# Block products of weights that stay in PSUM, sums of weights made by transfers, and six more pairs of products done by blocks

## The chip, the cores and the metric

The kernel runs on one core of one Trainium2 chip. The metric is the device time of one execution in microseconds (us); three executions before the change took 1703.23, 1706.94 and 1707.2 us, a median of 1706.94 us. The engines are TensorE (PE, with its weight loads as PEld), VectorE (DVE), ScalarE (ACT), GpSimd (POOL) and SyncE (SP, which here only issues transfers).

## The reference, cut to what matters

A decoder trunk of two layers runs on 512 prompt tokens and 64 sample tokens (8 sequences of 8), so 576 columns in all, with a model width of 1024 and a branch width of 2048, in float32. Layer 0 is a gated short convolution, layer 1 an mLSTM block. What matters here are the products with weight matrices:

```python
# layer 0
b_gate, c_gate, xa, z = jnp.split(h @ w_in, 4, axis=-1)      # 1024 -> 4 * 2048
u = c_gate * xa
conv, new_buf = causal_dwconv(u, buf, conv_w)
y = b_gate * conv * jax.nn.silu(z)
x = x + y @ w_out                                            # 2048 -> 1024
# layer 1
xm, z = jnp.split(h @ w_in, 2, axis=-1)                      # 1024 -> 2 * 2048
xc = silu(causal_dwconv(xm, ...) + conv_b)
q, k, v = xc @ w_q, xc @ w_k, xm @ w_v                       # 2048 -> 2048 each
...                                                          # gates, chunkwise mLSTM, states
x = x + ((norm(h) * onorm_w + skip * xc) * silu(z)) @ w_out
```

All twelve outputs (both token groups' results, the new convolution states, and the mLSTM's states) are computed by both kernels.

## The kernel before, in words

**Tiles.** Activations lie with the width on the 128 partitions and the 576 tokens along the row. A weight chunk is the weights of 128 output columns for 1024 inputs, 128 x 1024 values (512 KB), loaded as one tile `wr`. Every float32 operand is split in two parts of fewer bits, `hi` (a cast on ACT) and `lo` (the rest, a subtraction on DVE), and a product is three matmuls: hi by hi, hi by lo, lo by hi. `split_weights` (lines 208 and 209) and `parts_of` (lines 256 and 257) do this for weights, half a chunk (128 x 512) at a time, into rings of four `wh` and four `wl` tiles.

**Plain products.** `products` (matmuls on line 228) multiplies one chunk with 8 input tiles: 8 x 3 x 2 = 48 matmuls, since the 576 tokens are done as 256 and 320 columns.

**Block products.** `block_pair` (matmuls on line 310) does two chunks at once by Winograd's form of Strassen's method. The two chunks by the two halves of the input tiles are four weight blocks a11, a12, a21, a22; the inputs are cut the same way, by halves of the tiles and of the tokens (288 each), and their sums t1 to t4 are made once (`mixed`). Seven products of 12 matmuls with 288 columns, 84 in all, take the place of the 96 of two plain products. The sums of weights are made on DVE: s1 = a21 + a22 and s2 = s1 + a11 (lines 292 and 293), a21 + a11 (line 326) and s2 + a12 (line 331). Four PSUM banks of the tag `blk` hold the products; between them, results go to SBUF and are combined there by additions on DVE (lines 322 to 359).

**Layer 0.** A loop runs over 16 width tiles f. In each, the gate and input chunks of the next tile (4f+4 and 4f+5) are done by `block_pair`; then the last two chunks of this tile, 4f+2 for z and 4f+3 for the output gate, by two plain products (`product(2)` and `product(3)`). The convolution's steps of the tile stand in a list `work` and are let in between the blocks. In layer 0, tiles of the tag `X` (7 buffers) hold the sums and intermediate results; the loads have 4 `wr` buffers.

**Layer 1.** After the projection, `gemm_pair` computes v (8 pairs) and then k and q (16 pairs): for each pair a block product of 84 matmuls for the lower 1024 inputs, and two calls of `plain` (line 369), 48 matmuls each, which add the upper 1024 inputs in the same PSUM banks. `then` names the next pair, whose weights are loaded and summed from within this one. Behind these come the mLSTM's chunks, the z products and the output product; `block_pair` has no part in them.

**What sets the order.** The program is written in one order, and a scheduler that models the time of each instruction puts each engine's queue in order when the kernel is built. Each queue is then worked through in order, with semaphore waits. SP's queue issues the loads of the weights, in order too: a load that waits for its buffer holds up the ones behind it.

Of the kernel before, what the change touches and what calls it, by code (L numbers as in the profile page):

```python
# [57 lines left out]
AHEAD = 2  # L58
FH = 2
FI = 1  # L60
EARLY = 3.45
# [6 lines left out]
def trunk(tc, io):  # L68
    nc = tc.nc
    ctx = ExitStack()  # L70
    with ctx:
# [150 lines left out]
        def step(acc, w, xs, k, first, last, parts=HALVES):  # L222
# [3 lines left out]
            for p, (a, x) in enumerate(((hi, xh), (hi, xl), (lo, xh))):  # L226
                for i, j, o in parts:
                    nc.tensor.matmul(acc[:, o:o + j - i], a[:, k % 4, :], x[:, i:j], start=(first and k == 0 and p == 0),  # L228
                                     stop=(last and k == 7 and p == 2))

        def products(acc, w, xs, first, last, pops=(), parts=HALVES, hook=None):


            fence = nullcontext
            for k in range(8):
                if hook and hook[0] == k:
                    ins = hook[1]()
                    fence = lambda: tc.issue_after(ins)
                with fence():
                    step(acc, w, xs, k, first, last, parts)  # L240
                if k in pops:
                    run()
                tick(0.735 if len(parts) == 2 else 0.36)

# [37 lines left out]

        ahead_of = {}

        def block_weights(c1, c2):

            r1, r2 = weight_tile(), weight_tile()
            for r, c_ in ((r1, c1), (r2, c2)):
                latest[0] = load(out=r, in_=io["wts"][c_]).ins
            a11, a12, a21, a22 = [r[:, i:8:2, :] for r in (r1, r2) for i in range(2)]  # L290
            s1, s2 = [X(512, name="ws").rearrange("p (k x) -> p k x", x=P) for _ in range(2)]
            nc.vector.tensor_tensor(s1, a21, a22, ALU.add)
            nc.vector.tensor_tensor(s2, s1, a11, ALU.add)
            ahead_of[c1, c2] = a11, a12, a21, a22, s1, s2

        def block_pair(c1, c2, fs, xs, out1, out2, add, mid=None, then=None, pops=0):

            a11, a12, a21, a22, s1, s2 = ahead_of.pop((c1, c2))  # L300
            o11, o12, o21, o22 = out1[:, 0:HT], out1[:, HT:NT], out2[:, 0:HT], out2[:, HT:NT]
# [15 lines left out]
            nc.scalar.copy(p, b0)  # L317
            run(pops)
            b2 = block("p5")
            product(b2, parts_of(s1), "t1", True)  # L320
            if add:
                tt(o12, o12, b1, ALU.subtract)
                tt(o12, o12, p, ALU.add)
            else:
                tt(o12, p, b1, ALU.subtract)
            tt(a21, a21, a11, ALU.add)
            product(b1, parts_of(a21), "t3", False)
            run(pops)
            tt(u, b1, p, ALU.subtract)
            product(b0, parts_of(a12), "b21", False)  # L330
            tt(s2, s2, a12, ALU.add)
            if add:
                tt(o22, o22, b2, ALU.subtract)
                tt(o22, o22, u, ALU.add)
            else:
                tt(o22, u, b2, ALU.subtract)
            run(pops)
            b3 = block("p4")
            product(b3, parts_of(a22), "t4", True)
            run(pops)  # L340
            product(b2, parts_of(s2), "b22", False)
            if mid:
                mid()
            if then:
                block_weights(*then)
            if add:
                tt(o11, o11, b0, ALU.add)
                tt(o21, o21, b3, ALU.add)
                tt(o21, o21, u, ALU.add)
            elif xs is None:  # L350
                nc.scalar.copy(o11, b0)
                tt(o21, b3, u, ALU.add)
            else:
                plain(b3, b1, c2 + 1, xs, False)
                tt(o21, b3, u, ALU.add)
                tt(o22, b1, o22, ALU.add)
                plain(b0, b2, c1 + 1, xs, None)
                nc.scalar.copy(o11, b0)
            tt(o12, o12, b2, ALU.add)

        def plain(ba, bb, chunk, xs, start):

            w = weights(chunk)
            for k in range(8):
# [6 lines left out]
                if k % 2:  # L371
                    run()
                    drip()

        def gemm_pair(c1, c2, fs, xs, out1, out2, plain_first=False, mid=None, then=None):
# [159 lines left out]
        for f in range(NW):  # L535
# [17 lines left out]

            zb = [raw_weights(4 * f + i) for i in (2, 3)] if f else None
            if f + 1 < NW:
                cx = [X(name="cx") for _ in range(2)]
            if f == 0:
                for i in range(2):
                    acc = mm("acc")
                    products(acc, weights(4 + i), h1, True, True)  # L560
                    nc.scalar.copy(cx[i], flat(acc))
                    if i:
                        block_weights(8, 9)
                    first_blocks(2 + i)
                accumulators("acc0a", bufs=2)
            elif f + 1 < NW:
                block_pair(4 * f + 4, 4 * f + 5, fs, None, *cx, False, pops=1)
# [15 lines left out]
            nc.vector.tensor_tensor(cv, product(3), cv, ALU.mult)  # L583
            nc.vector.tensor_tensor(cv, cv, z, ALU.mult)
# [34 lines left out]
        for f in range(NW):  # L619
# [4 lines left out]
            if f < 2:  # L624
                u = raws[f]
                nc.vector.tensor_tensor(u, u, rb, ALU.mult)
            else:
                acc = gemm(80 + f, 1, h2)
                u = T(name="xm")
                nc.vector.tensor_tensor(u, flat(acc), rb, ALU.mult)  # L630
            us.append(u)
# [70 lines left out]
        xc, fc = [], []  # L702
        accumulators("acc1", bufs=4)

        def later_tile(f):
# [3 lines left out]

        def mixed_blocks():  # L710
            for j in range(4):
                fc.append(forms(later_tile(2 * j), later_tile(2 * j + 1)))

        for h in range(NH):
            vt = []
            for dt in (0, 2):
                f = 4 * h + dt
                pair = [T(name="v") for _ in range(2)]
                gemm_pair(96 + 2 * f, 98 + 2 * f, fm, xm, *pair, mid=mixed_blocks if f == NW - 2 else None,
                          then=(100 + 2 * f, 102 + 2 * f) if f < NW - 2 else (176, 178))  # L720
# [98 lines left out]
        for h in (3, 0, 1, 2):  # L819
            st = heads[h]  # L820
            for dt in range(4):
# [11 lines left out]
                if (h, dt) == (2, 3):  # L833
                    xs = []
                gemm_pair(128 + 4 * f, 130 + 4 * f, fc, xc, k, q, plain_first=(h, dt) == (3, 0),
                          mid=next_stage if (h, dt) == (2, 3) else None,
                          then=next(((128 + 4 * g, 130 + 4 * g) for i, g in enumerate(order) if i and order[i - 1] == f), None))
# [676 lines left out]
def _arrays(a):  # L1514
# [91 lines left out]
```

## Time and profile before

| | us |
|---|---|
| median of three executions | 1706.94 |
| the profiled execution's own time | 1710.66 |
| its span, from the first to the last instruction | 1708.8 |
| PE busy | 1670.7 (98% of the span) |
| DVE busy | 1094.3 (64%) |
| ACT busy | 682.3 (40%) |
| POOL busy | 102.3 (6%) |

A busy PE says little on how well it is used, since the matmuls overlap; the time from one matmul's start to the next's says more. The profile's chain of waits follows the work back from the end of the kernel, so a stage in which it names PE alone is one in which nothing but the number of matmuls and their rate sets the time. Line numbers (L310) are those of the kernel before; the same matmuls stand on L332 in the changed one, `parts_of` on L268 and L269 and `plain` on L407.

### The profile page before, as it was taken

What the parts mean: (1) busy time and instruction counts of PE and PEld (TensorE: products, weight loads), DVE (VectorE), ACT (ScalarE), POOL (GpSimd) and SP (SyncE); (2) the same over time, 40 slices, a digit from 0 to 9 for tenths busy, and PEclk for the clock granted to TensorE, in tenths of its full rate; (3) what the DMA queues carried; (4) which work ended last, traced back from release to release, by engine and by line L of the source; (5) the groups of instructions that cost most, each with busy time, mean ns of one, the idle gap of its engine ahead of it and who ended that gap; (6) DMA issues with size and microseconds to landing.
All of it is one profiled execution on the core that took longest, in us unless ns stands there. A gap on an engine that the chain in (4) does not pass through costs nothing.

```text
span 1708.8 us, 30842 instructions
## 1 busy us (share of the span) xinstructions
PE 1670.7 (98%) x12315; PEld 1592.4 (93%) x12315; DVE 1094.3 (64%) x2040; ACT 682.3 (40%) x1252; POOL 102.3 (6%) x241
## 2 busy tenths in 40 slices
PE   9999999999999999999999999999999998997998
PEld 9999999999999999999999989899898787997998
DVE  6977777774436986556856346345368567776775
ACT  5433343342323553433534223233245455554431
POOL 0000000000001000000110110000012000000000
PEclk9999999999999999999999999999999899998999
DMA  5223322224432434445433453542746587897993
GB/s 194 74 80 103 101 89 81 94 74 137 131 121 87 145 111 150 130 133 163 139 93 121 178 181 96 201 160 75 248 153 200 183 284 272 300 341 259 325 332 105
DMA packets 107487, 275.23 MB, mean 161 GB/s; under 512 B 11056, under 2 KB 33456, under 8 KB 107344
## 3 DMA queue, kind: packets, MB, share of 16 engines
q1 hardware_dynamic: 91984, 255.95, 45.4%
q10 hardware_dynamic: 15360, 17.32, 3.0%
q8 instruction: 97, 1.59, 0.4%
q14 instruction: 46, 0.38, 0.1%
HBM read 211.13 MB, written 62.09 MB: 160 GB/s over the span
## 4 chain that ended last, share of the span: by engine, by line
PE 89%; DMA 5%; DVE 3%; ACT 1%; issue 1%; POOL 1%; SPq 0%; DVEq 0%; ACTq 0%
PE acc L228 35%; PE p L310 24%; PE p L369 16%; DMA c<-cs 2%; PE qa L768 2%; DMA cs_out<-c 2%; PE cp L1183 1%; PE r L1129 1%; PE cp L1184 1%; PE g L669 1%; PE ta L688 1%; PE blk L369 1%; PE s L787 1%; DMA wr<-wts 1%; PE s L788 0%
## 5 line engine op out<-in xcount | busy, mean ns | idle before, releaser
L228 PE MATMUL acc<-hi,wh 128*128 128x256 f32 (+1 forms) x1520 | 331.5, 298 | 6.6 <-ACT num L1196 3.6
L208 ACT CAST wh<-wr 128x512 fp32r<-128x512 f32 x286 | 175.9, 620 | 390.9 <-PE acc L228 193.8
L228 PE MATMUL acc<-lo,wh 128*128 128x256 f32 (+1 forms) x1520 | 328.6, 297 | 0.0
L228 PE MATMUL acc<-hi,wl 128*128 128x256 f32 (+1 forms) x1520 | 328.5, 297 | 0.0
L310 PE MATMUL p<-hi,wh 128*128 128x288 f32 x968 | 286.1, 298 | 4.3 <-ACT wh L256 2.1
L310 PE MATMUL p<-lo,wh 128*128 128x288 f32 x968 | 284.4, 295 | 0.0
L209 DVE TENSOR_TENSOR wl<-wr,wh 128x512 fp32r<-128x512 f32 x286 | 194.1, 687 | 137.8 <-ACT wh L208 131.0
L310 PE MATMUL p<-hi,wl 128*128 128x288 f32 x968 | 277.9, 296 | 0.0
L228 PEld LDWEIGHTS acc<-hi,wh 128*128 128x128 f32 x1520 | 256.9, 190 | 12.5 <-ACT num L1196 3.8
L228 PEld LDWEIGHTS acc<-lo,wh 128*128 128x128 f32 x1520 | 255.9, 190 | 1.9 <-issue 1.7
L228 PEld LDWEIGHTS acc<-hi,wl 128*128 128x128 f32 x1520 | 255.9, 190 | 0.4
L310 PEld LDWEIGHTS p<-hi,wh 128*128 128x128 f32 x968 | 181.9, 188 | 7.4 <-ACT wh L256 3.9
L310 PEld LDWEIGHTS p<-lo,wh 128*128 128x128 f32 x968 | 182.4, 188 | 0.0
L310 PEld LDWEIGHTS p<-hi,wl 128*128 128x128 f32 x968 | 179.7, 189 | 1.9 <-issue 1.7
L256 ACT CAST wh<-wr 128x512 fp32r<-128x512 f32 x152 | 94.3, 621 | 217.7 <-PE p L369 97.9
L369 PE MATMUL p<-hi,wh 128*128 128x288 f32 x736 | 168.5, 299 | 0.0
L369 PE MATMUL p<-hi,wl 128*128 128x288 f32 x736 | 167.2, 297 | 0.0
L369 PE MATMUL p<-lo,wh 128*128 128x288 f32 x736 | 165.4, 295 | 0.0
L257 DVE TENSOR_TENSOR wl<-wr,wh 128x512 fp32r<-128x512 f32 x152 | 104.6, 688 | 53.1 <-ACT wh L256 52.1
L257 DVE TENSOR_TENSOR wl<-ws,wh 128x512 fp32r<-128x512 f32 x114 | 78.6, 689 | 89.3 <-ACT wh L256 82.1
L256 ACT CAST wh<-ws 128x512 fp32r<-128x512 f32 x114 | 70.7, 620 | 154.5 <-PE p L369 69.4
L369 PEld LDWEIGHTS p<-hi,wh 128*128 128x128 f32 x736 | 120.4, 188 | 12.6 <-issue 9.4
(367 smaller groups left out, 2542.4 us busy)
## 6 DMA issues: line engine op xcount, KB each, us to landing
wr<-wts SPq DMA_DIRECT2D x222, 512.0 KB, 3.9
c<-cs SPq DMA_DIRECT2D x112, 512.0 KB, 6.1
cs_out<-c SPq DMA_DIRECT2D x64, 512.0 KB, 6.9
x<-xT SPq DMA_DIRECT2D x16, 288.0 KB, 4.2
xcs<-xc ACTq DMA_DIRECT2D x16, 288.0 KB, 2.1
x<-xcs SPq DMA_DIRECT2D x16, 288.0 KB, 4.7
ld<-xcs SPq DMA_DIRECT2D x16, 288.0 KB, 7.2
cp_out<-cp ACTq DMA_DIRECT2D x16, 257.0 KB, 7.2
```

The source lines that it names most:

```text
L208: last_act[0] = nc.scalar.copy(hi, raw[:, 4 * i:4 * i + 4, :]).ins
L209: nc.vector.tensor_tensor(lo, raw[:, 4 * i:4 * i + 4, :], hi.bitcast(F32), ALU.subtract)
L228: nc.tensor.matmul(acc[:, o:o + j - i], a[:, k % 4, :], x[:, i:j], start=(first and k == 0 and p == 0), stop=(last and k == 7 and p == 2))
L256: last_act[0] = nc.scalar.copy(hi, src).ins
L257: nc.vector.tensor_tensor(lo, src, hi.bitcast(F32), ALU.subtract)
L310: nc.tensor.matmul(bank_, a[:, j, :], x, start=(start and j == 0 and i == 0), stop=(j == 3 and i == 2), skip_group_check=True)
L369: nc.tensor.matmul(b, a[:, k % 4, :], x[:, t:t + HT], start=bool(new) and k == 0 and i == 0, stop=(k == 7 and i == 2), skip_group_check=True)
L669: nc.tensor.matmul(g[32 * j:32 * j + 32, 0:b - a], w[:, 32 * j:32 * j + 32], tiles[j][:, a:b], start=True, stop=True)
L688: nc.tensor.transpose(pa[:, 128 * it:128 * it + 128], t[:, 128 * it:128 * it + 128], ident)
L768: nc.tensor.matmul(st["q"][32 * g:32 * g + 32, :], st["qp"][dt // 2][:, dt % 2, 128 * u + 32 * g:128 * u + 32 * g + 32], ct[g // 2][:, g % ...
L787: nc.tensor.matmul(sb[0], a[:, 0:128], b[:, 0:512], **ends)
L1129: nc.tensor.matmul(r, kst[2 * i + j][:, 128 * dt:128 * dt + 128], vst[:, 0:512], start=True, stop=True)
```

## The change

Four things are changed.

1. **Chained products.** The products of a pair are put in another order, and the partial sums stay in PSUM. ACT writes the negative of the first product (a11 by b11) into a second bank, and three further products accumulate there one after another; ACT copies the partial sums out in between (`u`, then `p`, or the fourth bank `bv` where plain products follow). DVE makes two subtractions with results in place of five operations. Since a matmul that is to add onto what ACT wrote needs the bank to have been written by a matmul before, `mark` writes all four banks once by four matmuls of 288 columns where a new set of banks is opened: in layer 0 and ahead of layer 1's v.
2. **Sums by transfers.** For all pairs but the first of layer 0 and the first of layer 1 (`FIRST`), s1 is made by a load of a21 (SP) and an accumulating transfer of a22 onto it (POOL's queue), and a21 + a11 by an accumulating transfer of a11 onto a21. DVE still makes s2 = s1 + a11 and s2 + a12. The accumulating transfers are issued later than the loads (`settle`). The chunks of block products are stored in another order in HBM, so that a block is one piece.
3. **Six tiles' last two products by blocks.** In the width tiles 3, 5, 7, 9, 11 and 13 of layer 0 (`SECOND`), the chunks 4f+2 and 4f+3 are done by a second `block_pair` and no longer by two plain products.
4. **Small things.** The result tiles `cx` come from the large pool for f under 11; the last two projection tiles of layer 1 leave PSUM by an ACT copy; a job between two pairs (`mixed_blocks`) is let in in four pieces.

```diff
+FIRST = (8, 96)
+SECOND = tuple(range(3, 14, 2))
...
+        add_load = nc.gpsimd.dma_start
...
+        def settle():
+            while unsettled:
+                unsettled.pop(0)()
...
         def block_weights(c1, c2):
             r1, r2 = weight_tile(), weight_tile()
             for r, c_ in ((r1, c1), (r2, c2)):
                 latest[0] = load(out=r, in_=io["wts"][c_]).ins
-            a11, a12, a21, a22 = [r[:, i:8:2, :] for r in (r1, r2) for i in range(2)]
+            a11, a12, a21, a22 = [r[:, i:i + 4, :] for r in (r1, r2) for i in (0, 4)]
             s1, s2 = [X(512, name="ws").rearrange("p (k x) -> p k x", x=P) for _ in range(2)]
-            nc.vector.tensor_tensor(s1, a21, a22, ALU.add)
-            nc.vector.tensor_tensor(s2, s1, a11, ALU.add)
+            if c1 in FIRST:
+                nc.vector.tensor_tensor(s1, a21, a22, ALU.add)
+                nc.vector.tensor_tensor(s2, s1, a11, ALU.add)
+                nc.vector.tensor_tensor(a21, a21, a11, ALU.add)
+            else:
+                load(out=s1, in_=io["wts"][c2][:, 0:4, :])
+                def sums():
+                    add_load(out=s1, in_=io["wts"][c2][:, 4:8, :], accum_op=ALU.add)
+                    add_load(out=a21, in_=io["wts"][c1][:, 0:4, :], accum_op=ALU.add)
+                    nc.vector.tensor_tensor(s2, s1, a11, ALU.add)
+                unsettled.append(sums)
...
-            b1 = block("p6")
-            product(b1, parts_of(s2), "t2", True)
-            b0 = block("p1")
-            product(b0, parts_of(a11), "b11", True)
-            nc.scalar.copy(p, b0)
...
+            bx = block("p1")
+            product(bx, parts_of(a11), "b11", True)
+            by = block("p6")
+            nc.scalar.activation(by, bx, AF.Copy, scale=-1.0)
+            bw = block("p5")
+            product(bw, parts_of(s1), "t1", True)
+            m5 = X(HT, name="m5")
+            nc.scalar.copy(m5, bw)
+            product(by, parts_of(s2), "t2", False)
+            nc.scalar.copy(u, by)
+            tt(s2, s2, a12, ALU.add)
+            product(bx, parts_of(a12), "b21", False)
+            product(by, parts_of(a21), "t3", False)
+            if xs is None or add:
+                nc.scalar.copy(p, by)
+            else:
+                bv = block("p7")
+                nc.scalar.copy(bv, by)
+            product(bw, parts_of(s2), "b22", False)
+            product(by, parts_of(a22), "t4", False)
...
+            if xs is None:
+                tt(o22, p, m5, ALU.subtract)
+                nc.scalar.copy(o11, bx)
+                tt(o12, bw, u, ALU.subtract)
+                nc.scalar.copy(o21, by)
+                return
+            plain(bx, bw, c1 + 1, xs, None)
...
+        def mark(w, x):
+            for b in [block("mark") for _ in range(4)]:
+                nc.tensor.matmul(b, w, x, start=True, stop=True)
...
+            second = f in SECOND
+            if second:
+                block_weights(4 * f + 2, 4 * f + 3)
...
-            za = product(2)
             z = T(name="z")
+            if second:
+                b_ = T(name="b")
+                block_pair(4 * f + 2, 4 * f + 3, fs, None, z, b_, False)
+                za = z
+            else:
+                za = product(2)
             nc.vector.tensor_tensor(z, za, rb, ALU.mult)
...
+    blk = [c for c in range(64) if (c // 4 in SECOND if c % 4 > 1 else c >= 8)] + list(range(96, 192, 2))
+    wts[blk] = wts[blk][:, :, [0, 2, 4, 6, 1, 3, 5, 7]]
```

How the queues' order moves is shown at three places. The first is PE's queue in layer 0, in width tile f = 3, where the pair of the next tile ends and the work on z and the output gate begins. Before (`p6183` is a bank of the pair, `acc198` the accumulator of z):

```order
L310 MATMUL p6183_1250<-hi109_664,wh189_1306 128x288
L310 MATMUL p6183_1250<-lo110_665,wh189_1306 128x288
L310 MATMUL p6183_1250<-hi109_664,wl189_1307 128x288
L228 MATMUL acc198_1393<-hi14_137,wh199_1394 128x256
L228 MATMUL acc198_1393<-hi14_137,wh199_1394 128x320
L228 MATMUL acc198_1393<-lo15_138,wh199_1394 128x256
```

and now (`p6191` belongs to the pair of the next tile, `p1207` is the first bank of the new second pair):

```order
L332 MATMUL p6191_1286<-hi109_665,wh197_1347 128x288
L332 MATMUL p6191_1286<-lo110_666,wh197_1347 128x288
L332 MATMUL p6191_1286<-hi109_665,wl197_1348 128x288
L332 MATMUL p1207_1417<-hi14_137,wh208_1418 128x288
L332 MATMUL p1207_1417<-lo15_138,wh208_1418 128x288
L332 MATMUL p1207_1417<-hi14_137,wl208_1419 128x288
```

Where 96 matmuls of line 228 stood, 84 of 288 columns stand. The second place is POOL's queue in layer 0, in which before nothing stood but one small copy for each width tile (`cpa`):

```order
L547 COPY cpa_501<-u83_504 128x2
L547 COPY cpa_501<-u114_691 128x2
L547 COPY cpa_501<-u145_966 128x2
L547 COPY cpa_501<-u176_1241 128x2
L547 COPY cpa_501<-u208_1519 128x2
```

and in which now the accumulating transfers stand between them (L310 and L311 are lines of the changed kernel; `ws` is s1, `wr` the chunk that holds a21):

```order
L587 COPY cpa_501<-u149_977 128x2
L310 DMA ws169_1125<-wts 128x512
L311 DMA wr168_1122<-wts 128x512
L310 DMA ws184_1260<-wts 128x512
L311 DMA wr183_1257<-wts 128x512
L587 COPY cpa_501<-u180_1254 128x2
L310 DMA ws202_1408<-wts 128x512
L311 DMA wr201_1405<-wts 128x512
```

Each of these waits on POOL for the loads of the tiles onto which it adds. The third place is ACT's queue at the new second pair of f = 3, as it is now (`wh` are casts of weights, `p6209` is the bank that is chained, `pu206` and `m5212` take its partial sums and the fifth product's, and `cx187`, a result of the pair before, its last):

```order
L268 CAST wh214_1473<-wr182_1256 128x512
L338 ACTIVATE p6209_1434<-p1207_1417 128x288
L268 CAST wh215_1489<-wr183_1257 128x512
L377 COPY cx187_1264<-p6191_1286 128x288
L268 CAST wh216_1506<-ws185_1261 128x512
L343 COPY m5212_1453<-p5210_1436 128x288
L268 CAST wh217_1522<-wr183_1257 128x512
L346 COPY pu206_1416<-p6209_1434 128x288
L268 CAST wh229_1563<-wr200_1404 128x512
```

Between two copies out of, or into, a bank stands one cast of a later product's weights in most places; before, a pair had two such copies on ACT in all, and now it has six.

More of the change, by code (lines that the diff above doesn't have):

```diff
@@ L242, in products @@
                     run()
+                if k == 5 and unsettled:
+                    settle()
                 tick(0.735 if len(parts) == 2 else 0.36)
@@ L346, in block_pair @@
             if add:
[L347 to L359, printed above, removed]
+                tt(p, p, m5, ALU.subtract)
+                tt(o22, o22, p, ALU.add)
+                tt(o12, o12, u, ALU.subtract)
+                tt(o12, o12, bw, ALU.add)
+                tt(o11, o11, bx, ALU.add)
+                tt(o21, o21, by, ALU.add)
+                return
[4 more added lines that the diff above has]
+                nc.scalar.copy(o21, by)
+                return
+            plain(bx, bw, c1 + 1, xs, None)
+            nc.scalar.copy(o11, bx)
+            if mid:
+                nc.scalar.copy(o12, bw)
+            tt(o12, o12 if mid else bw, u, ALU.subtract)
+            for go in mid[2:3]:
+                go()
+            plain(by, bv, c2 + 1, xs, None)
+            nc.scalar.copy(o21, by)
+            if mid:
+                nc.scalar.copy(o22, bv)
+            tt(o22, o22 if mid else bv, m5, ALU.subtract)
+            for go in mid[3:]:
+                go()
+        def mark(w, x):
+            for b in [block("mark") for _ in range(4)]:
+                nc.tensor.matmul(b, w, x, start=True, stop=True)
         def plain(ba, bb, chunk, xs, start):
@@ L552, in trunk @@
             work.append(saved)
-            zb = [raw_weights(4 * f + i) for i in (2, 3)] if f else None
+            second = f in SECOND
+            if second:
+                block_weights(4 * f + 2, 4 * f + 3)
+            zb = [raw_weights(4 * f + i) for i in (2, 3)] if f and not second else None
             if f + 1 < NW:
-                cx = [X(name="cx") for _ in range(2)]
+                cx = [T(name="cx") if f < 11 else X(name="cx") for _ in range(2)]
             if f == 0:
@@ L577, in product @@
                 return flat(acc)
-            za = product(2)
             z = T(name="z")
+            if second:
[4 more added lines that the diff above has]
+                za = product(2)
             nc.vector.tensor_tensor(z, za, rb, ALU.mult)
             nc.scalar.activation(z, z, AF.Silu)
-            nc.vector.tensor_tensor(cv, product(3), cv, ALU.mult)
+            nc.vector.tensor_tensor(cv, b_ if second else product(3), cv, ALU.mult)
             nc.vector.tensor_tensor(cv, cv, z, ALU.mult)
@@ L629, in trunk @@
                 u = T(name="xm")
-                nc.vector.tensor_tensor(u, flat(acc), rb, ALU.mult)
+                if f < NW - 2:
+                    nc.vector.tensor_tensor(u, flat(acc), rb, ALU.mult)
+                else:
+                    nc.scalar.copy(u, flat(acc))
+                    nc.vector.tensor_tensor(u, u, rb, ALU.mult)
             us.append(u)
@@ L708, in later_tile, with mixed_blocks @@
             return x
-        def mixed_blocks():
-            for j in range(4):
-                fc.append(forms(later_tile(2 * j), later_tile(2 * j + 1)))
+        def mixed_blocks(j):
+            fc.append(forms(later_tile(2 * j), later_tile(2 * j + 1)))
         for h in range(NH):
@@ L718, in trunk @@
                 pair = [T(name="v") for _ in range(2)]
-                gemm_pair(96 + 2 * f, 98 + 2 * f, fm, xm, *pair, mid=mixed_blocks if f == NW - 2 else None,
+                gemm_pair(96 + 2 * f, 98 + 2 * f, fm, xm, *pair, mid=[lambda j=j: mixed_blocks(j) for j in range(4)] if f == NW - 2 else None,
                           then=(100 + 2 * f, 102 + 2 * f) if f < NW - 2 else (176, 178))
```

36 lines of the change are left out of this document (12 added, 24 removed).

## Prediction

> **What bounds the kernel now.** I read the head of the page first, with the shares of the chain of waits by engine.
>
> ```profile
> span 1708.8 us, 30842 instructions
> PE 1670.7 (98%) x12315; PEld 1592.4 (93%) x12315; DVE 1094.3 (64%) x2040; ACT 682.3 (40%) x1252; POOL 102.3 (6%) x241
> PE 89%; DMA 5%; DVE 3%; ACT 1%; issue 1%; POOL 1%; SPq 0%; DVEq 0%; ACTq 0%
> ```
>
> PE carries 89% of the chain. Next come four stretches in the view of windows: twelve width tiles of layer 0, layer 1's v pairs, its k and q pairs, and the rest.
>
> ```profile
> core 0: us, PE busy (x) PEld busy (x) DVE busy (x) ACT busy (x) POOL busy (x), PEclk, DMA share, GB/s
> 101.25:387.16 285.91, 285.91 (x2154) 285.91 (x2154) 215.69 (x380) 112.63 (x192) 7.00 (x12) 1.00 0.29 89
> 612.00:833.40 221.40, 219.70 (x1697) 216.15 (x1697) 146.86 (x281) 93.41 (x166) 11.69 (x33) 1.00 0.45 143
> 833.40:1290.00 456.60, 453.08 (x3394) 417.64 (x3398) 231.69 (x409) 150.76 (x272) 52.37 (x129) 1.00 0.46 150
> 1290.00:1708.80 418.80, 393.37 (x2713) 357.62 (x2707) 289.10 (x584) 193.70 (x409) 16.28 (x36) 0.96 0.76 261
> ```
>
> In layer 0 PE is busy for all of 285.91 us at full clock: only fewer or shorter matmuls help there. The 677 us of v, k and q hold 5.2 us in which PE is free. Last, the chain in one width tile of layer 0, where the pieces are start, length, line and count:
>
> ```profile
> 101.25 9.52 PE p L310 x72
> 110.77 4.92 PE acc L228 x37
> 115.69 1.59 PE p L310 x12
> 117.28 7.88 PE acc L228 x59
> ```
>
> A pair by blocks is 9.52 + 1.59 = 11.11 us for 84 matmuls (0.132 us each), the two plain products are 4.92 + 7.88 = 12.80 us for 96. Together they are the tile's 23.91 us.
>
> **Second pairs.** Six tiles lose 96 matmuls each and gain 84: 12.80 - 11.11 = 1.69 us, times 6 is **-10.14 us**, if the second pair runs as close as the first. Lower bound of the gain 0 (the pair waits for its weights as long as it saves), upper bound the sum itself.
>
> **Opening of the first pair.** This is the one place ahead of layer 0's loop where PE stands still. The timeline on PE and ACT, and three windows behind it:
>
> ```profile
> 48.41 0.42 PE L228 MATMUL acc<-hi,wl 128*128 128x256 f32 x2
> 50.91 0.40 PE L310 MATMUL p<-hi,wh 128*128 128x288 f32 x1 [2.08 <-ACT wh L256]
> 48.87 0.64 ACT L561 COPY cx<-acc 128x576 f32<-128x576 f32 x1 [1.92 <-PE acc L228]
> 50.90:52.80 1.90, 1.89 (x8) 1.25 (x9) 1.90 (x4) 1.90 (x4) 0.00 (x0) 1.00 0.03 9
> 52.80:56.30 3.50, 3.50 (x17) 3.50 (x16) 3.50 (x7) 0.81 (x2) 0.10 (x1) 0.51 0.01 2
> 56.30:57.00 0.70, 0.70 (x8) 0.70 (x7) 0.43 (x1) 0.21 (x1) 0.48 (x1) 1.00 0.00 0
> ```
>
> Before, the pair opens with the sum s2, behind two additions and a cast. Now it opens with a11 and b11, which need no sum; only the four marks wait for the copy `cx`, which ends at 49.51. Four marks are 4 x 0.132 = 0.53 us, so the first product starts near 50.1 in place of 50.91: **-0.8 us**. After the stall the clock is granted at 0.51 for 3.5 us, 3.5 x 0.49 = 1.7 us lost. Whether a shorter stall spares it no row shows: between 0 and -1.7 I take half, **-0.85**.
>
> The Trainium skill (TensorE: Matmul & The Clock Gate, Part 1) has the clock fall only after a whole idle window of about 3.4 us. This trace disagrees, since it fell after 2.08 us. By the page the new, shorter stall could cost nothing, and the sum would be 0.85 us lower.
>
> **Marks ahead of v.** Here PE waits for the last projection tile:
>
> ```profile
> 611.25 0.77 DVE xm L630
> 612.16 9.76 PE p L310 x72
> ```
>
> The new ACT copy (0.64 us by `cx` above) stands ahead of that multiplication, but the marks need only the first tile and may fill the wait. Between 0 and +0.53 I take **+0.53**. The banks are then in use; later pairs have no marks.
>
> **Sums by transfers.** 42 pairs get a third load on SP and two transfers on POOL in place of two additions on DVE. No transfer that adds stands in the trace; the nearest rows are loads in layer 0 (first) and transfers of 256 KB among layer 1's k and q, median us to landing last; and POOL's small operations:
>
> ```profile
> wr<-wts SPq DMA_DIRECT2D x51, 512.0 KB, 3.6
> kps<-ta ACTq DMA_DIRECT2D x15, 256.0 KB, 3.2
> far<-S SPq DMA_DIRECT2D x3, 256.0 KB, 6.5
> ld<-vps SPq DMA_DIRECT2D x1, 256.0 KB, 10.1
> L547 POOL COPY cpa<-u 128x2 f32<-128x2 f32 x12 | 7.0, 584 | 276.6 <-DVE u L544 276.6
> L744 POOL TENSOR_TENSOR qm<-q,nst 128x64 f32<-128x64 f32 x16 | 13.8, 860 | 307.1 <-DVE q L356 284.1 <-DVE q L334 23.0
> L293 DVE TENSOR_TENSOR ws<-ws,wr 128x512 f32<-128x512 f32 x11 | 7.6, 692 | 0.4
> L256 ACT CAST wh<-wr 128x512 fp32r<-128x512 f32 x47 | 29.2, 622 | 57.0 <-PE acc L228 39.3 <-PE p L310 17.7
> ```
>
> The new chain is: chunk load 3.6, load of s1 behind it at most 3.6, POOL's issue 0.58 to 0.86, the transfer A, DVE's s2 0.69, ACT's cast 0.62: 9.4 us + A by the longer values. By the queues' order there lie, in some 18 pairs of layer 0, at least 123 matmuls between the last one that the load waits for and the first that needs what stands behind the sum: 123 x 0.132 = 16.3 us. So A may take 6.9 us before PE waits. Bounds for A are 3.2 and 10.1; layer 0's DMA share is 0.29 against 0.46 where the long ones are, so I take the 3.6 of its own loads: **0**, hidden behind the preceding pair's matmuls. At 10.1 it would be 18 x 3.2 = 57 us. In layer 1 the distances are longer, but for one (105 matmuls, 13.9 us, at the first k and q pair); the third load stands there on SP ahead of the `c` loads, for which PE waits 2.5 us now:
>
> ```profile
> PE qa L768 <- DMA c<-cs: 2.5, 3, 1.4
> ```
>
> Doubled that is +2.5; fewer DVE operations could give back at most the 5.2 us; between these I take 0.
>
> **Chained products.** DVE loses work, ACT gains four operations in a pair. Rows of layer 0:
>
> ```profile
> L317 ACT COPY pu<-p 128x288 f32<-128x288 f32 x12 | 4.7, 393 | 0.0
> L438 ACT ACTIVATE cv<-u,cols 128x576 f32<-128x576 f32 x12 | 9.3, 774 | 0.0
> L352 DVE TENSOR_TENSOR cx<-p,pu 128x288 f32<-128x288 f32 x12 | 5.4, 450 | 0.0
> L257 DVE TENSOR_TENSOR wl<-wr,wh 128x512 fp32r<-128x512 f32 x47 | 32.2, 685 | 1.8 <-ACT wh L256 0.8
> ```
>
> Each of these copies has one whole product, 12 matmuls or 1.59 us, between its bank's last matmul and the next one that adds there. A copy with one operation ahead of it on ACT is at most 0.77 + 0.39 = 1.17 us, which is covered; with two, 0.77 + 0.62 + 0.39 = 1.79 us, it is 0.2 us late, and behind the waiting matmul stand all others. ACT is busy 112.63 of 285.91 us, 39%, so I take **0**; three late copies in each of 44 pairs would be 3 x 44 x 0.2 = 26 us.
>
> **DVE where it is densest.** A second tile has 22.22 us (two pairs) in place of 23.91. DVE's 215.69 us over 285.91 are 18.04 in a tile. Four subtractions for plain weights go (-2.74), seven for blocks come (+4.80), the first pair loses two sums (-1.37) and three of five 288-wide operations (-1.35), the second brings two sums (+1.37) and two subtractions (+0.90): 19.65 of 22.22 us, 88%. It fits, with little room.
>
> **The last stage** (1290 on) has none of these products. Only its order on the queues moves a little; I take 0, with 2 us either way.
>
> **Sum.** -10.14 - 0.8 - 0.85 + 0.53 = **-11.26 us**. The profiled execution took 1710.66 us, 1.86 over its span, and stands 3.72 above the median; so 1699.40 for it, and **1695.7** for the median.
>
> **Rivals.**
>
> *R1, the sums come late (slower).* Layer 0, some 18 pairs: it decides from A = 6.9 us on. For it speak the rows of 6.5 and 10.1 us at the same size; against it the light DMA there and the 3.2. At 10.1 us: 1695.7 + 57 = 1753; at 7.5 it would still be 1706.5.
>
> *R1b, POOL's issue is held up by DVE.* If POOL could prepare a transfer only while DVE is free, 12% of a second tile, its 0.86 us would become 0.86 / 0.12 = 7.2, the chain 15.7 us + A, and with A = 3.6 PE would wait 3.0 us: x 18 = 54, some 1750. Against it: the small POOL copy takes 584 ns beside a DVE that is busy 75%. The Trainium skill (SBUF — State Buffer, The "DVE blocks DMA" trap) states such a lock, for DVE's two-port modes; no run here shows it yet.
>
> *R2, copies late on the chained bank (slower).* Price above: 1695.7 + 26 = 1722. For it: more ACT operations in the same bank's path; against it: ACT's 39%.
>
> *R3, the second pairs give nothing.* With DVE at 88%, the `lo` parts come when the matmuls want them, and the tile keeps its 23.91 us: 1695.7 + 10.14 = 1705.8. For it: the density; against it: DVE's idle time in layer 0 waits for ACT and PE, not the reverse.
>
> *R4, more gain.* The whole clock loss (-0.85) and most of the 5.2 us of PE's free time in v, k and q: some 1690.
>
> **How the numbers follow.** A measurement tells 0.3% from no change, so faster is under 1701.8 and slower over 1712.1. Forecast 0.64 (1691 to 1701.8), R4 0.06: faster 0.70. R3 0.13, all of it within: same 0.13. R1 0.09, R1b 0.03, R2 0.05: slower 0.17. The range is 1689 to 1709: it holds the forecast, R3 and most of R4, and leaves out the slower cases, 0.17, as its remainder. Their prices begin near nothing, so some of them would fall inside as well.
>
> **What would show it.** In the changed profile: two pairs of 84 in width tiles 3, 5, ... 13 with PE unbroken, such a tile 22.2 us long where a plain one stays at 23.9; PE's groups fewer by 64 matmuls; the first pair's stall under 1.3 us and the window behind it at a clock over 0.51; the transfers `ws<-wts` on POOL's queue landing under 6.9 us; no wait of PE on ACT for the chained bank over 0.2 us. I am wrong if layer 0's twelve tiles show PE idle by more than 2 us for `ws`, for the bank's copy or for `wl`; the releaser named there tells R1, R2 and R3 apart.

## The result and the profile after

The changed kernel is slower by 0.4%: a median of 1713.4 us against 1706.68 (15 executions each), a ratio of 1.0037 with a 95% interval of 1.0027 to 1.0047. Forecast were 1695.7 us, in a range of 1689 to 1709. In a second series, on chip 11, the ratio came to 1.0030 (1.0016 to 1.0045).

The head of the profile after (1711.83 us, 1.6 under its median, where before's 1710.66 stood 4.0 over its own) still shows PE as the chain, with the share of transfers up from 5% to 8%:

```profile
span 1710.1 us, 31151 instructions
PE 1673.2 (98%) x12251; PEld 1583.8 (93%) x12251; DVE 1026.3 (60%) x1873; ACT 749.8 (44%) x1463; POOL 168.6 (10%) x325
PE 86%; DMA 8%; DVE 3%; ACT 2%; issue 1%; SPq 1%; POOL 0%; DVEq 0%; ACTq 0%
```

Layer 0 did what was forecast. In the chain of the changed kernel's first dense tiles, 240 block matmuls follow one another without a gap (a pair, the second pair, and six of the seven products of the next tile's pair), and two width tiles take 144.97 - 98.82 = 46.15 us where two took 47.82 before:

```profile
98.82 31.76 PE p L332 x240
130.58 3.59 PE acc L231 x27
134.16 1.59 PE p L332 x12
135.76 9.21 PE acc L231 x69
144.97 31.76 PE p L332 x240
```

Layer 1's first block product comes at 602.05 us (before: 612.16). The 10.1 us are gone again when v, k and q are done. Here is that stage, from the first block product to the last gate product, as the view of windows has it, before and then after:

```profile
612.16:1294.30 682.14, 677.08 (x5132) 636.85 (x5132) 380.44 (x692) 244.73 (x438) 63.97 (x162) 1.00 0.46 149
```

```profile
602.05:1296.21 694.16, 688.63 (x5120) 637.21 (x5119) 320.69 (x550) 274.61 (x539) 94.99 (x207) 1.00 0.58 171
```

It is 12.0 us longer with 12 matmuls fewer, at full clock, and PE is busy for 11.6 us more of it. So it isn't idle time, which goes from 5.1 to 5.5 us: the same instructions take longer. The groups by line tell which; first before, then after (busy us, mean ns, waits):

```profile
L768 PE MATMUL qa<-c,qp 128*32 128x512 f32 x192 | 25.6, 604 | 2.5 <-DMA c<-cs 2.5
L669 PE MATMUL g<-k,wif 128*32 128x256 f32 (+1 forms) x64 | 8.1, 417 | 0.0
L669 PE MATMUL g<-v,wif 128*32 128x256 f32 (+1 forms) x64 | 4.7, 412 | 0.3 <-DVE tb L693 0.3
L669 PE MATMUL g<-q,wif 128*32 128x256 f32 (+1 forms) x64 | 4.7, 412 | 0.0
```

```profile
L821 PE MATMUL qa<-c,qp 128*32 128x512 f32 x192 | 30.8, 605 | 2.2 <-DMA c<-cs 2.1
L722 PE MATMUL g<-k,wif 128*32 128x256 f32 (+1 forms) x64 | 11.5, 416 | 0.0
L722 PE MATMUL g<-v,wif 128*32 128x256 f32 (+1 forms) x64 | 6.4, 415 | 0.0
L722 PE MATMUL g<-q,wif 128*32 128x256 f32 (+1 forms) x63 | 4.9, 413 | 0.0
```

Neither line was edited. `qa` is the query's product with the states, `g` the gates' product; both use 32 of the array's columns (128*32), four of them side by side. They grew by 5.2 and 5.3 us, 10.5 of the 12.0. The timeline shows why (a *run* of small matmuls is here a row of them on PE with no other matmul between). Before, eight `qa` in a row take 1.06 us and sixteen `g` 1.18:

```profile
965.92 1.06 PE L768 MATMUL qa<-c,qp 128*32 128x512 f32 x8
678.51 1.18 PE L669 MATMUL g<-v,wif 128*32 128x256 f32 x16
```

In the changed kernel large matmuls stand between them, and a run of two costs what a run of eight did:

```profile
959.97 1.06 PE L821 MATMUL qa<-c,qp 128*32 128x512 f32 x6
963.26 1.04 PE L821 MATMUL qa<-c,qp 128*32 128x512 f32 x2
660.56 0.63 PE L722 MATMUL g<-v,wif 128*32 128x256 f32 x4
662.89 0.63 PE L722 MATMUL g<-v,wif 128*32 128x256 f32 x4
664.17 0.73 PE L722 MATMUL g<-v,wif 128*32 128x320 f32 x2
670.86 0.74 PE L722 MATMUL g<-v,wif 128*32 128x320 f32 x6
```

In PE's order there are 38 runs of `qa` for 33 in the whole kernel and 28 of `g` for 19. In v, k, q alone `qa` has 29 runs for 24, and the number of runs accounts for its whole growth: 24 runs of 1.06 to 1.07 us are the 25.6 us of before, 29 are the 30.8 of now. The scheduler lets a small product in where its inputs are ready by its model, and the changed pair has its results ready at other times; which part of the change broke the runs is tested below, while the model's own times are not on record.

### The profile page after: what moved, and what is told of

It is laid out like the page before. It is cut to its first block, busy times and chain, and to the rows that moved or that the text cites. A ratio compares the mean times of both kernels' runs of the same rounds, so it can differ in the third digit from the quotient of the medians.

```text
span 1710.1 us, 31151 instructions
## 1 busy us (share of the span) xinstructions
PE 1673.2 (98%) x12251; PEld 1583.8 (93%) x12251; DVE 1026.3 (60%) x1873; ACT 749.8 (44%) x1463; POOL 168.6 (10%) x325
## 4 chain that ended last, share of the span: by engine, by line
PE 86%; DMA 8%; DVE 3%; ACT 2%; issue 1%; SPq 1%; POOL 0%; DVEq 0%; ACTq 0%
PE acc L231 29%; PE p L332 28%; PE p L407 16%; DMA cs_out<-c 2%; PE qa L821 2%; DMA wr<-wts 2%; DMA c<-cs 2%; PE r L1182 1%; PE g L722 1%; PE cp L1236 1%; PE cp L1237 1%; PE ta L741 1%; PE s L840 1%; DMA ws<-wts 1%; PE s L841 0%
## 5 line engine op out<-in xcount | busy, mean ns | idle before, releaser
L332 PE MATMUL p<-hi,wh 128*128 128x288 f32 x1136 | 337.0, 297 | 0.8 <-ACT p L355 0.4
L332 PE MATMUL p<-hi,wl 128*128 128x288 f32 x1136 | 334.7, 295 | 0.7 <-DVE wl L269 0.7
L332 PE MATMUL p<-lo,wh 128*128 128x288 f32 x1136 | 334.4, 295 | 0.0
L231 PE MATMUL acc<-hi,wh 128*128 128x256 f32 (+1 forms) x1328 | 290.0, 299 | 5.7 <-ACT num L1249 2.4
L231 PE MATMUL acc<-lo,wh 128*128 128x256 f32 (+1 forms) x1328 | 288.8, 298 | 0.0
L231 PE MATMUL acc<-hi,wl 128*128 128x256 f32 (+1 forms) x1328 | 288.2, 298 | 0.0
L231 PEld LDWEIGHTS acc<-hi,wh 128*128 128x128 f32 x1328 | 224.7, 191 | 11.5 <-issue 2.6
L231 PEld LDWEIGHTS acc<-hi,wl 128*128 128x128 f32 x1328 | 224.2, 191 | 2.1 <-issue 1.7
L231 PEld LDWEIGHTS acc<-lo,wh 128*128 128x128 f32 x1328 | 224.5, 191 | 0.8 <-issue 0.6
L332 PEld LDWEIGHTS p<-hi,wl 128*128 128x128 f32 x1136 | 212.9, 188 | 3.2 <-issue 2.1
L407 PE MATMUL p<-hi,wh 128*128 128x288 f32 x736 | 161.4, 300 | 0.0
L407 PE MATMUL p<-hi,wl 128*128 128x288 f32 x736 | 160.3, 297 | 0.0
L407 PE MATMUL p<-lo,wh 128*128 128x288 f32 x736 | 159.2, 295 | 0.0
```

What stands on the lines that cost most here:

```text
L332: nc.tensor.matmul(bank_, a[:, j, :], x, start=(start and j == 0 and i == 0), stop=(j == 3 and i == 2), skip_group_check=True)
L407: nc.tensor.matmul(b, a[:, k % 4, :], x[:, t:t + HT], start=bool(new) and k == 0 and i == 0, stop=(k == 7 and i == 2), skip_group_check=True)
```

## The experiments

Two theories stand against each other at first: O, that the order of the small products in layer 1 took the gain; and S, that the sums by transfers come late and hold PE up. Every kernel's stages are read from its trace: "start" to layer 1's first block product, "v, k, q" to the last gate product, "last" to the end of the span. The ratio is to the kernel before on the same chip.

| kernel | ratio (95%) | start | v, k, q | last |
|---|---|---|---|---|
| before | 1 | 612.2 | 682.1 | 414.5 |
| changed | 1.0037 (1.0027 to 1.0047) | 602.0 | 694.2 | 413.8 |
| changed, again | 1.0030 (1.0016 to 1.0045) | 601.8 | 692.5 | 411.3 |
| no second pairs | 1.0106 (1.0080 to 1.0132) | 611.4 | 693.9 | 416.1 |
| before with second pairs | 0.9987 (0.9972 to 1.0003) | 614.0 | 680.3 | 410.9 |
| layer 0 only | 0.9932 (0.9911 to 0.9952) | 603.3 | 680.3 | 406.6 |
| glued | 0.9978 (0.9962 to 0.9993) | 605.2 | 681.6 | 415.4 |
| glued, fourth head as it was | 0.9962 (0.9947 to 0.9977) | 603.5 | 682.3 | 409.0 |
| old form with transfers in layer 1 | 0.9973 (0.9961 to 0.9986) | 603.6 | 690.2 | 411.7 |
| all sums on DVE | 0.9978 (0.9962 to 0.9993) | 601.0 | 685.4 | 408.5 |
| layer 0 only, glued | 0.9889 (0.9871 to 0.9907) | 602.8 | 676.0 | 403.5 |
| layer 0 only, glued, sums on DVE | 0.9873 (0.9853 to 0.9894) | 600.2 | 676.8 | 406.6 |
| chained, glued, sums on DVE | 0.9930 (0.9910 to 0.9949) | 601.1 | 680.6 | 409.7 |
| before, glued | 0.9984 (0.9970 to 0.9999) | 610.7 | 678.6 | 409.8 |

**The second pairs undone.**

```diff
-SECOND = tuple(range(3, 14, 2))
+SECOND = ()
```

> The changed kernel with SECOND empty: the last two products of all width tiles of layer 0 by plain products; the rest as changed. Theory O (order: layer 1's stage of v, k and q got longer because the small matmuls of 32 columns stand in more and shorter runs on PE; layer 0 gained what was forecast): the six tiles give back 10.1 us, so 1713.4 + 10 = 1723 us, ratio to before 1.009 to 1.011. Theory S (sums late: the accumulating transfers hold PE up in layer 0's dense tiles in most executions): without the dense tiles those stalls go too, so 1713 to 1718. Theory D (second pairs give nothing, R3): 1713.

The start is 9.3 us longer (8.4 from the first block product on) and v, k, q as long as in the changed kernel: the second pairs bring what was forecast of them but for 1 to 2 us, and have no part in the loss. Of these 1 to 2 us, 1.1 are PE's idle time in the dense tiles of the changed kernel, busy for 275.13 of 276.20 us from 98.80 on, where here it is busy for all of them. The median is 1722.27, as O and the forecast's first term have it.

**The second pairs alone**, in the kernel before (and with the result tiles `cx` in the large pool, as in the changed kernel).

```diff
+            second = f in SECOND
+            if second:
+                block_weights(4 * f + 2, 4 * f + 3)
...
+                block_pair(4 * f + 2, 4 * f + 3, fs, None, z, b_, False)
```

> The kernel before with the six second pairs alone: old form of the block product, sums on DVE, no chaining, no transfers that add. PE's order in layer 1 is that of before (33 groups of rows for the 32-column products of the query with the states, as before; 38 in the changed kernel). Theory O: -10.1 us in layer 0 and nothing lost later, 1696 to 1698, ratio 0.994. Theory D: DVE is over its limit in the dense tiles with the old form (18.04 - 2.74 + 4.80 + 5.0 for the second pair's four sums and five operations = 25.1 us against 22.2), so the tile is bound by DVE at about 25 us: 1706.7 + 6 x 1.2 = 1714.

Here the start gained nothing, and the 1703.16 us are neither O's 1696 to 1698 nor D's 1714. PE's waits in the dense tiles (us in total, times, longest) name the old form's chain on DVE and ACT:

```profile
PE p L311 <- DVE pu L330: 4.4, 3, 2.2
PE p L311 <- ACT pu L318: 3.4, 4, 0.9
```

Line 330 is the subtraction `u`, which reads the bank that a next product needs. So rival R3 holds for the old form, with DVE at 240.17 of 276.20 us (87%) over these tiles: its operations come late before it is full on average. With chaining the second pairs pay, and it needs no transfers for that (the run with all sums on DVE, below).

**Layer 0 as changed, layer 1's pairs as before**: sums on DVE, and `old_pair`, which is the block product of before written out again.

```diff
-            if c1 in FIRST:
+            if c1 >= 96:
+                nc.vector.tensor_tensor(s1, a21, a22, ALU.add)
+                nc.vector.tensor_tensor(s2, s1, a11, ALU.add)
+            elif c1 in FIRST:
...
-            block_pair(c1, c2, fs, xs, out1, out2, plain_first, mid, then)
+            old_pair(c1, c2, fs, xs, out1, out2, plain_first, mid, then)
...
-        mark(xm[0][0][:, 0:P], xm[0][0][:, 0:HT])
```

> The changed kernel in layer 0 (chained products, sums by transfers, second pairs), with layer 1's pairs by the block product of before and their sums on DVE, and no marks ahead of v. PE's runs of small matmuls are those of before. Theory O: layer 0's gain stays, layer 1's loss goes: 1706.7 - 10.8 = 1696, ratio 0.993 to 0.995. Theory S: what makes the changed kernel's median 5.5 us longer against its profile than before's is layer 0's transfers, so 1700 to 1703.

1692.65 us: the forecast's size, from the part of the change that the forecast's first terms were about. All that was lost lies in layer 1's edits and behind them: v, k, q are 13.9 us shorter than in the changed kernel. Not all of the gain is the start, which fell by 8.9 us; part of it is in the last stage, which is open (below).

**The small products put together again.** Two steps of `qa` become one job of eight, and `g` begins with the tile and half that come last.

```diff
-            for g in (2, 3, 0, 1):
+            if i % 2 == 0:
+                st["ct"] = ct
+                return
+            for m, ct_ in ((i, ct), (i - 1, st["ct"])):
...
-            for a, b, _ in HALVES:
+            for a, b, _ in reversed(HALVES):
...
-                for j in range(4):
+                for j in (3, 2, 1, 0):
```

> The changed kernel with the small matmuls of layer 1 put in an order that keeps them together: two steps of the query's product with the states are issued as one job of eight, the one whose states are loaded last first (the sums are the same in another order), and the gates' products begin with the tile and the half that come last. The groups of rows on PE go from 38 to 23 for qa and from 28 to 24 for g. Theory O: each broken run costs about one round of 0.45 us and two switches of about 0.1, so qa's 4.85 us come back and some 10 switches x 0.25 more, g some 1: -6 to -9 us, 1704 to 1707, ratio 0.999 to 1.001. Theory S: nothing there, 1712 to 1714.

In this kernel the fourth head's deferred step reads a state that has been updated, so that head's sample outputs are others than the reference's; the work is the same. v, k, q fell from 694.2 to 681.6. The next run leaves that head as it was.

> The changed kernel with the same grouping as before in the glued run for the first three heads and the gates, while the fourth head's steps, which run among the updates of the states, stay as they were. Theory O: layer 1's stage 694.2 -> 681 to 683, the time as in the glued run, ratio 0.997 to 0.999. Rival (the glued run was short because its fourth head was in another order too): 1.000 to 1.003.

682.3 us and 1699.51 in all. The window of v, k, q and the row of `qa` in this run:

```profile
603.48:1285.75 682.27, 675.70 (x5120) 636.69 (x5119) 320.39 (x550) 273.68 (x537) 96.95 (x207) 1.00 0.58 174
L827 PE MATMUL qa<-c,qp 128*32 128x512 f32 x192 | 23.1, 598 | 4.1 <-DMA c<-cs 4.0
```

PE does as many matmuls as in the changed kernel (5120) and is busy for 12.9 us less, 7.7 of them in `qa` and 2.9 in `g` (19.9 us in all for 22.8). So 12 us come back by the order of the two small products alone, more than the 6 to 9 that O expected. Part of it is new gain: `qa` is then in runs of 16, which in an order that wasn't broken bring 4.3 us too (680.3 to 676.0, below). Some 8 us are the broken runs, the greater part of layer 1's loss; 6.3 against the 676.0 stay.

**What broke the runs: chaining or transfers.** Layer 1 in the old form, with transfers:

```diff
+            if c1 in FIRST:
+                tt(a21, a21, a11, ALU.add)
...
-            block_pair(c1, c2, fs, xs, out1, out2, plain_first, mid, then)
+            old_pair(c1, c2, fs, xs, out1, out2, plain_first, mid, then)
```

> Layer 0 as changed; layer 1's pairs by the block product of before, not chained, but with their sums made by transfers as in the changed kernel, no marks ahead of v. On PE qa has 33 groups of rows as before (38 in the changed kernel), g 23 (19 before, 28 changed). Theory O (the chained form's results come one by one, and the scheduler lets the small products in as they come): layer 1's stage 681 to 683, ratio 0.993 to 0.996. Theory S (transfers cost in layer 1): the stage at 690 or more, ratio over 0.998.

and everything chained, without transfers:

```diff
-FIRST = (8, 96)
+FIRST = tuple(range(192))
```

> The changed kernel with all sums of weights on DVE (FIRST holds all pairs): chained products and second pairs stay, no transfer adds. In a dense tile DVE then has 18.04 - 2.74 + 4.80 - 1.35 + 2.74 + 0.90 = 22.4 us of work in 22.2: it is the bound. From the first block product to layer 1's first one: 551 us in the changed kernel, 561 before, 563 with second pairs in the old form; here 553 to 557. Layer 1's stage 694, since the chained form breaks the runs (qa has 39 groups of rows): some 1715 to 1719, ratio 1.005 to 1.008. If the transfers were the cost: layer 1's stage under 688, ratio under 1.001.

With the two kernels above, this is a square for v, k, q: old form and DVE sums 680.3, transfers alone 690.2, chaining alone 685.4, both 694.2. Both of my theories were half right: by these single executions transfers cost 9 to 10 us there and chaining 4 to 5. The values are less sure than they look. The profile of the transfers alone is of an execution 6.9 us over its median, and by the ratios of the medians (0.9973 against 0.9932 with layer 0 only) transfers cost some 7 us; with the changed kernel's second profile (692.5) they cost 7.1 and chaining 2.3. So transfers cost 7 to 10 us and chaining 2 to 5. They work in different ways. Chaining alone breaks `qa`; its row in the run with all sums on DVE:

```profile
L821 PE MATMUL qa<-c,qp 128*32 128x512 f32 x192 | 31.8, 605 | 1.0 <-DMA c<-cs 1.0
```

Transfers alone leave `qa` whole (24 runs, 25.6 us), but PE waits longer for its states' loads, among which the third loads of the pairs now stand in SP's queue. In the old form with transfers, and then in the run with layer 0 only:

```profile
PE qa L888 <- DMA c<-cs: 3.9, 6, 1.5
PE g L790 <- DVE tb L814: 1.4, 1, 1.4
```

```profile
PE qa L888 <- DMA c<-cs: 0.5, 1, 0.5
PE g L790 <- DVE tb L814: 0.3, 1, 0.3
```

That is 3.4 + 1.1 us; `g`, in 23 runs, adds 2.0, and the rest of the 9.9 is spread over matmuls between the small groups. How much of the 3.4 is the transfers' stays open: before's own profile, without transfers, has 2.5 us of this wait, and the changed kernel's 2.1. In layer 0 the sums on DVE cost nothing: the start is 601.0 us, a little better than with transfers, and DVE at 229.66 of 276.20 us (83%) holds nothing up: PE is busy for all 276.20. I had expected DVE to be the bound there.

**What is left if the parts that pay are kept.** Layer 0 as changed, layer 1 as before, `qa` of three heads in jobs of eight. The edit turns the gates' order round too, although the expectation says that they stay as they are:

> Layer 0 as changed, layer 1's pairs as before (as in the run with layer 0 only), and the small matmuls of the query with the states for the first three heads issued as jobs of eight, the step whose states come last first; 24 runs of 8 in the trace become 12 of 16 in the order, the gates' products stay as they are. Theory O: a run costs two switches, in all some 0.25 us, beyond its rounds, so 12 x 0.25 = 3 us come off layer 1's stage (680.3 to about 677.5) and off the time: ratio 0.991 to 0.992. Rival: a job of eight needs four state tiles at once, and the waits for the loads `c` grow by as much: no change against 0.9932.

the same with every sum on DVE (`FIRST = tuple(range(192))`), so with no transfer that adds:

> No transfer that adds anywhere: chained products and second pairs in layer 0 with their sums on DVE, layer 1's pairs in the form of before with sums on DVE, the query's products with the states of three heads in jobs of eight. Its stages as the earlier runs had them: up to layer 1's first block product 549.5 (run with all sums on DVE), layer 1's stage 676.0 (layer 0 glued), the rest as in that run: 1687.0 - 1.4 = 1685.6, ratio 0.987 to 0.989. Rival (the transfers in layer 0 are free but for one late sum, and DVE at 83% pays elsewhere): 1687 to 1690.

1683.36 us, 1.3% under the kernel before, is the fastest of all. One of its `qa` rows reads

```profile
960.16 1.92 PE L894 MATMUL qa<-c,qp 128*32 128x512 f32 x16
```

Sixteen in 1.92 us against twice 1.06: a join saves 0.2 us and the switch around it, and there are 12 of these runs for 24 of eight. `qa` takes 23.1 us in v, k, q for 25.6, while `g` has 19 runs as without the edit (17.6 us for 17.5). The kernel before with this grouping (and the gates' order) alone:

> The kernel before with nothing but the jobs of eight (three heads) and the gates' order. In the run with layer 0 only this took 4.3 us off layer 1's stage (680.3 to 676.0) and 5.6 off the time. Theory O: as much here, 1706 to 1701, ratio 0.996 to 0.998. Rival (it pays only with the changed layer 0): 0.999 to 1.001.

gains 0.16%. Of the 1.3%, a little over half (0.68%) is there with layer 0 only, which brought the chained second pairs; the grouping added 0.43% to that (0.16% in the kernel before), and sums on DVE in place of transfers 0.16%, which is inside the intervals. And chaining everywhere, with jobs of eight and sums on DVE:

> The changed kernel with all sums on DVE and with the jobs of eight: chained products everywhere, second pairs, no transfers that add. Layer 1's stage was 694.2 as changed, 682.3 with the jobs of eight, 685.4 with sums on DVE. Theory O: the two act on the same runs of small matmuls in part; the chained form alone costs nothing, so 676 to 679 and a ratio of 0.990 to 0.993. Rival (the chained form's copies on ACT hold PE up in layer 1, R2): 682 or more, ratio over 0.995.

v, k, q took 680.6, between both expectations, and the ratio is O's: `qa` still stands in 24 runs in the whole kernel (21 in the fastest). On the same chip its median is 10.3 us over the fastest kernel's, so chaining in layer 1 brings nothing here either; 3.8 us of that lie in v, k, q, and the rest is not assigned.

**The changed kernel once more.**

> The changed kernel once more, on the chip of the runs beside it. Open is the last stage, from layer 1's last gate product to the end: 413.8 us in its first profile, 406.6 and 410.9 in two kernels whose order there is that of before, and 414.5 in before's own profile, which was 4 us over its median. If the last stage of the changed order is longer by itself, this profile has it at 412 to 416 again (adjusted by what the profiled time differs from the median), with 50 loads of state tiles in it up to the last state product against 48. If it was chance: 405 to 411. The stages ahead of it: 551 and 694 within 2 us. Ratio 1.002 to 1.005.

The stages ahead repeat (601.8 and 692.5), and the last one is 411.3 in an execution 3.8 us under its median. The last stage moves 263 to 324 GB/s in its four middle parts of 70 us, before and after, and differs by several us between executions and kernels. The changed order has two state loads more in it, since two fewer are issued in v, k, q; the rows of v, k, q for these loads, before and after:

```profile
c<-cs SPq DMA_DIRECT2D x52, 512.0 KB, 5.9
```

```profile
c<-cs SPq DMA_DIRECT2D x50, 512.0 KB, 6.0
```

Two loads are 1.05 MB, at the 293 GB/s of the state updates 3.6 us. The start's gain (-8.8 to -10.2) and v, k, q (+10.4 to +12.0, and more against the 680.3 of other runs in before's order) leave some 2 to 6 us of the medians' 6.7 for the last stage, of which these loads would explain the greater part. All seven profiles of kernels chained in layer 1 have 62 of the loads in the last stage and take 408.5 to 416.1 us there; the seven others have 60 and take 403.5 to 414.5. The ranges overlap, and no run takes the loads out alone, so this part stays open.

## Why the prediction was wrong, point by point

The start came out near the forecast, -10.1 us for -11.26. The step that failed is layer 1, where the prediction put "Chained products" and "Sums by transfers" at 0 each because it found no wait that they would cause. The runs showed +12.0 us in v, k, q in their place, of which PE's idle time is 0.5 us: 10.5 us of it is `qa` and `g`, which nobody edited, in more and shorter runs.

**Second pairs, -10.14: right.** 9.3 us by the run without them; 11.2 us of the start (612.2 to 601.0) with all sums on DVE, 1.5 of which is the clock, below.

**Opening, -0.8 - 0.85: wrong in both parts.** The start of the first product moved by 0.1 us. The copy that frees the banks stands on ACT behind two casts, and the marks wait for it:

```profile
48.42 0.62 ACT L268 CAST wh<-wr 128x512 fp32r<-128x512 f32 x1 [0.57 <-PE acc L231]
48.94 0.67 ACT L162 CAST hi<-fb 128x576 fp32r<-128x576 f32 x1
49.52 0.63 ACT L604 COPY cx<-acc 128x576 f32<-128x576 f32 x1
50.20 0.80 PE L397 MATMUL mark<-hi 128*128 128x288 f32 x4 [1.61 <-ACT cx L604]
```

I had taken the copy's place from before's order, where it was first. The clock's part came in full in this pair of profiles (1.00 in the changed one from 52.80 on), but no run shows that the shorter stall did it, and I count it as luck. In the run of before with the grouping alone, the same opening and the same wait are followed by full clock:

```profile
52.80:56.30 3.50, 3.50 (x28) 3.50 (x28) 3.50 (x7) 1.85 (x5) 0.01 (x1) 1.00 0.01 2
```

**Marks ahead of v, +0.53: right** (0.64 from the first mark at 601.41 to the first product at 602.05).

**Sums by transfers, 0: wrong.** In layer 0 the size was off and the limit right. The rows of layer 0's transfers (us to landing) and of POOL's issues:

```profile
ws<-wts SPq DMA_DIRECT2D x16, 256.0 KB, 3.9
ws<-wts POOLq DMA_DIRECT2D x16, 256.0 KB, 5.3
wr<-wts POOLq DMA_DIRECT2D x16, 256.0 KB, 4.1
```

```profile
L310 POOL DMA_DIRECT2D ws<-wts x16 | 14.8, 923 | 87.5 <-DVE wl L269 62.3 <-DMA ws<-wts 25.2
L311 POOL DMA_DIRECT2D wr<-wts x16 | 14.1, 879 | 60.5 <-DVE cx L376 14.3 <-DVE ws L312 11.4 <-DMA wr<-wts 10.4
```

A was 5.3 us in the median, not 3.6, and under the 6.9 from which PE would wait. Once, where the load itself took 5.5, the chain of waits goes through two transfers and PE lost 1.4 us (0.9 and 0.5 over the usual step), which happens to offset the 1.5 of the clock in the start:

```profile
320.64 5.49 DMA ws<-wts
326.13 0.40 issue
326.52 4.87 DMA ws<-wts
```

So R1 decided nothing in layer 0. R1b fell: an issue takes 0.88 to 0.92 us beside a DVE that is busy 76%, and not 7. The Trainium skill (DMA: Bandwidth & Descriptors, Anatomy of one DMA — SWDGE (gpsimd) path) puts a transfer of this queue at about 2.0 us and the bytes' time at 436 GB/s, by estimate 2.6 us for 256 KB; no run agrees, the transfers that add took 4.1 and 5.3 here. In layer 1, where I took 0 between +2.5 and -5.2, transfers cost 7 to 10 us. What failed there is the sentence "the third load stands there on SP ahead of the `c` loads": I priced the wait for `c` but not what else a queue's shift does to PE's order.

**Chained products, 0: wrong, and not by R2.** In v, k, q of the profile after PE waited once, 0.4 us, for a copy inside a pair, and 2.2 us ahead of the first k and q pair for the banks of the last v pair; in layer 0 it waited once, 0.35 us, for such a copy. Both waits are over the 0.2 us that I had named, but there are two of them, not three in each pair. The loss, 2 to 5 us in layer 1, came from the order: with chaining alone `qa` stands in 30 runs for 24. That results which are ready one by one draw the small products apart is my reading of it. The order itself was there before any run: 33 runs of `qa` against 38, 19 of `g` against 28. I quoted three places of the order in layer 0 and looked for waits in layer 1, and did not count the runs there.

**DVE where it is densest, 88%: right.** Over two tiles, one of them dense, its terms give 34.97 of 46.13 us, 76%, and DVE was busy 210.42 of 276.20 us, 76%. There is more room than I gave it, since nothing waited with all sums on DVE either; R3 happened only in the old form.

**The last stage, 0 with 2 us either way:** likely 2 to 6 us too low, as above; the cause stays open.

The cases left out another way to lose: nothing waits longer and nothing is full, but instructions that nobody touched stand in another order. (By the prediction's rows v, k and q are 678.0 us, not 677, which changes no term.) The sum that would have been right for the profiled pair of executions: -10.1 for the start, +12.0 for v, k, q, -0.7 for the last stage, +1.2 us.

## What to carry to other kernels

Where a scheduler orders the queues, compare the order in every stage whose code or inputs the change touches, and count the runs of small matmuls that use a part of the array's columns: here a broken run was a cost with no wait to show for it. The place to find it is the busy time of unchanged lines, stage by stage, not the list of waits. And take a change of four parts apart by stage: here one part was worth -10 us, and two others cost 12 to 14 in a place where they brought nothing.

## What the runs showed of the hardware

Matmuls that use 32 of the array's columns overlap with those beside them in a run: one of 512 columns takes 604 ns in the mean, but in v, k, q, at full clock, a run of 2, 4, 6 or 8 took 1.04 to 1.07 us and one of 16 took 1.92. In the single records of the trace a run of eight is four starts within 0.02 us and four more 0.45 us later; a run of two is two starts 0.45 us apart, and so as long. After a wait of 2.1 us on PE the clock was granted at 0.51 for 3.5 us in one execution and at 1.00 in another of the same opening; the Trainium skill (TensorE: Matmul & The Clock Gate, Part 1) asks for an idle window of about 3.4 us, which neither had. A transfer that adds onto SBUF, 256 KB from POOL's queue, landed after 4.1 to 5.3 us in layer 0, where a plain load of the same size took 3.9, and its issue held POOL 0.9 us.
